# A 224-byte tile dealt first from the right end of SBUF in a hybrid SSD/pool/ConvGLU block

## Chip, cores, metric

The kernel runs on one core of a Trainium2 chip. The metric is the device time of one execution in microseconds (us), lower is better.

## The reference, cut to what matters

One decoder block on a sequence of 1024 positions of width 1024, all in float32:

```python
u = rmsnorm(h, g_norm1) * (1 + scale1) + shift1
h = h + gate1 * hybrid_mixer(u, ...)
v = rmsnorm(h, g_norm2) * (1 + scale2) + shift2
h = h + gate2 * conv_glu(v, ...)
out = rmsnorm(h, g_final)
```

`hybrid_mixer` projects u to 8224 columns, convolves and gates them, runs a chunked state-space scan beside a multi-scale pooling branch, projects each branch back to width 1024, merges the two under sigmoid gates and multiplies by `w_out`. `conv_glu` projects v to 2 x 2816 columns, convolves one half, multiplies the halves, and projects back with `w_ffn_out`.

## The kernel before, in words

**Precision.** Every large product is made of three TensorE matmuls: a float32 operand is split into a high part in float32r (ScalarE, L133, L137 or L165) and a low part, the rest (VectorE or GpSimd, L134, L138 or L166), and high x high, high x low and low x high are added in PSUM. The matmul's stationary operand is a 128x128 piece of a weight form `wf`; the moving operand is a 128x512 half of an activation tile [128, 2, 512], 2048 bytes in each partition. Products in plain float32 exist too: the sums of squares (L482, L1049), the scan's products (L740 to L832), and a few small ones.

**Stages, in order of time.** (1) norm 1 and forms of u (to about 95 us); (2) the input projection, 31 pairs of column blocks by seven Winograd-style products each (`wino_pair`, L276, matmuls in `product`, L261), with an epilogue of convolution (L562 to L575) for most of the pairs; (3) the scan in chunks of 128 positions (L710 to L832), with the pooling branch's GEMMs (L877) and the first half of the SSD output projection (L905) filled in between by a hand-written table; (4) from about 1125 us the second half of that projection (moving operand `ya`, L993), the gates, and `w_out` (moving operand `mg`, L993); (5) residual, norm 2, forms of v (L1059 to L1108); (6) the FFN input projection, 22 pairs by `wino_pair` (moving operands `x..` and `xT..`, L261); (7) the FFN output projection (moving operand `hd`, L993), and the last norm.

**Where tiles lie.** SBUF is dealt out as a stack from each end of a partition. On the left lie `const`, `wp` (weights as loaded, `wr`, their sums, and the forms `wf`), `xf` (forms of u, `xa` and `xb`; stages 1 and 2) and `xp` (`pb`, then `ya` of the first half; stage 3). On the right lie, one after the other in time, `condp`, `xpool`, `cfp` and `evp` (stages 1 and 2), `sp`, `sl`, `sl2`, `sl3` (stage 3), and from stage 4 on `hp` and `slots`, from which every `ya`, `mg`, `x..`, `xT..`, `hd`, `h`, `gt`, `o` and `fin` tile is taken:

```python
    hp = ctx.enter_context(pool("hp", side="right"))
    sq_ = ctx.enter_context(pool("slots", side="right"))
    def take(shape, dtype, name):
        n = places.pop(0)
        t = sq_.tile(shape, dtype, name=name, tag=f"q{n}")
```

The right end from which tiles are dealt is byte 229,344 of a partition, which is 895 x 256 + 224. In the program before, every right-side tile therefore begins 224 bytes past a multiple of 256 (`ev` and `edge` at 160), since all but `edge` (64 bytes) have sizes that are multiples of 256. The left-side pools `wp`, `xf` and `xp` begin on multiples of 256, and so do all their tiles. `xf` reaches from byte 77,056 to 191,744; `slots` from 77,792 to 204,768. The PSUM banks of the large products are the same six before and after stage 3.

**Order of work.** The order on every engine is the program's order, but for two weight loads in stage 3 that are given a higher priority. A tile that takes the place of another waits for that one tile's last use (`reuse_waits="tile"`).

Of the kernel before, what the change touches and what calls it, by code (L numbers as in the profile page):

```python
# [9 lines left out]
F32 = mybir.dt.float32  # L10
# [6 lines left out]
P = 128  # L17
# [68 lines left out]
def block_kernel(ctx, tc, xT, ccol_d, crow, wadn, wada, prm_d, alog, dtbias, w_in, w_dt, w_grp, w_pout, w_sout, w_out, w_fin, w_fout,  # L86
# [28 lines left out]
    mod = const.tile([P, 48], F32, name="mod")  # L115
    gs1 = const.tile([P, 8], F32, name="gs1")
    gs2 = const.tile([P, 8], F32, name="gs2")
    cond_stack = ExitStack()
    cond = cond_stack.enter_context(tc.tile_pool(name="condp", bufs=1, side="right")).tile([P, 1024], F32, name="cond")

# [1145 lines left out]
```

## Time and profile before

| | us |
|---|---|
| median of 3 runs | 2031.9 |
| lowest and highest | 2030.55, 2033.45 |
| the profiled execution's own time | 2034.22 |
| its span, first to last instruction | 2032.4 |
| PE busy in it | 1888.7 (93%) |
| VectorE, ScalarE, GpSimd busy | 1352.2, 797.1, 694.7 |

The profile is of one execution. PE is TensorE's matmul record, PEld its weight load, DVE VectorE, ACT ScalarE, POOL GpSimd, SP the engine that issues most DMAs. Matmuls are pipelined: a record lasts longer than the time until the next one begins. So a run of n matmuls back to back lasts (n - 1) intervals and one record, and the interval is best read from the starts of two runs that follow each other. L-numbers are lines of the kernel.

### The profile page before, as it was taken

To read this page: it belongs to the slowest core of one execution; us is meant where nothing else is said; L and a number is where in the kernel's file an instruction comes from. 1 tells how busy PE (TensorE), PEld (TensorE's weight loads), DVE (VectorE), ACT (ScalarE), POOL (GpSimd) and SP (SyncE) were. 2 spreads that over 40 slices of the span, in tenths; PEclk is the share of its full clock that TensorE was granted. 3 is DMA by queue.
4 is the path that set the end of the run, shared out by engine and by line. 5 is a ranking of instruction groups with operands and counts; after the bars stand their busy time and mean duration, and the time that the engine had idled before them with its cause. 6 is when DMAs were issued, how large, how long until landed. Compare 5 with 4: busy or idle time off the path is not lost.

```text
span 2032.4 us, 23730 instructions
## 1 busy us (share of the span) xinstructions
PE 1888.7 (93%) x8480; PEld 1488.4 (73%) x8480; DVE 1352.2 (67%) x1863; ACT 797.1 (39%) x1299; POOL 694.7 (34%) x499
## 2 busy tenths in 40 slices
PE   4899999999899988987789999979999999999997
PEld 1477777777788866775567787757888888888885
DVE  7899998568754578877874444688676776723324
ACT  4545444333343374435532323454333333512211
POOL 4554545454554204544654001233232322000012
PEclk8899999999999999998899999989999999999998
DMA  7133343433343577778887545412222222634212
GB/s 310 53 129 135 125 141 130 152 121 118 134 141 129 180 236 223 218 215 236 270 249 233 174 135 175 156 52 97 90 73 84 75 81 89 206 105 129 80 36 83
DMA packets 163990, 294.65 MB, mean 145 GB/s; under 512 B 13344, under 2 KB 86176, under 8 KB 163360
## 3 DMA queue, kind: packets, MB, share of 16 engines
q1 hardware_dynamic: 142368, 276.36, 41.7%
q10 hardware_dynamic: 21504, 16.78, 2.6%
q8 instruction: 66, 1.08, 0.2%
q14 instruction: 52, 0.43, 0.1%
HBM read 221.92 MB, written 71.17 MB: 144 GB/s over the span
## 4 chain that ended last, share of the span: by engine, by line
PE 65%; DVE 15%; DMA 7%; issue 5%; POOL 4%; ACT 4%; SPq 0%; ACTq 0%; DVEq 0%; POOLq 0%
PE pg L993 21%; PE bz L261 16%; PE bx L261 11%; PE bw L261 11%; DVE acc L564 4%; DMA xs<-xbc_d 2%; PE q L905 2%; DVE wf L134 1%; DVE d L731 1%; POOL sq L812 1%; POOL yv L808 1%; DMA m_d<-ht 1%; ACT acc L562 1%; POOL yv L821 1%; PE q L877 1%
## 5 line engine op out<-in xcount | busy, mean ns | idle before, releaser
L155 POOL TENSOR_TENSOR wsum<-wr 128x512 f32<-128x512 f32 x108 | 171.5, 1588 | 302.2 <-DMA wr<-in_w_fin_dram 115.7
L993 PE MATMUL pg<-hd,wf 128*128 128x512 f32 x1056 | 247.7, 397 | 0.0
L993 PEld LDWEIGHTS pg<-hd,wf 128*128 128x128 f32 x1056 | 198.7, 188 | 48.4 <-issue 1.0
L134 DVE TENSOR_TENSOR wf<-wr,wf 128x512 fp32r<-128x512 f32 x198 | 174.9, 889 | 80.5 <-ACT wf L133 80.4
L133 ACT CAST wf<-wsum 128x512 fp32r<-128x512 f32 x216 | 132.2, 618 | 194.6 <-PE bz L261 174.7
L261 PE MATMUL bz<-xT,wf 128*128 128x512 f32 x792 | 197.8, 398 | 5.6 <-ACT xT L133 5.3
L261 PE MATMUL bz<-xb,wf 128*128 128x512 f32 x744 | 184.2, 397 | 13.3 <-DVE ev L294 13.3
L133 ACT CAST wf<-wr 128x512 fp32r<-128x512 f32 x198 | 121.8, 621 | 176.6 <-PE bw L261 134.3
L261 PEld LDWEIGHTS bz<-xT,wf 128*128 128x128 f32 x792 | 149.4, 189 | 43.6 <-ACT xT L133 6.0
L261 PEld LDWEIGHTS bz<-xb,wf 128*128 128x128 f32 x744 | 140.4, 191 | 48.7 <-DVE ev L294 19.8
L1057 POOL TENSOR_TENSOR total<-total,ht 128x512 f32<-128x512 f32 x20 | 32.7, 1639 | 412.6 <-ACT ht L1056 412.1
L134 POOL TENSOR_TENSOR wf<-wsum,wf 128x512 fp32r<-128x512 f32 x62 | 90.8, 1465 | 171.3 <-ACT wf L133 171.3
L165 ACT CAST wf<-wr 128x1024 fp32r<-128x1024 f32 (+2 forms) x64 | 58.4, 914 | 224.4 <-PE pg L993 180.6
L166 DVE TENSOR_TENSOR wf<-wr,wf 128x1024 fp32r<-128x1024 f32 (+2 forms) x64 | 71.3, 1119 | 112.6 <-issue 63.7
L261 PE MATMUL bx<-x,wf 128*128 128x512 f32 x528 | 132.9, 403 | 5.4 <-ACT ht L271 5.4
L134 DVE TENSOR_TENSOR wf<-wsum,wf 128x512 fp32r<-128x512 f32 x154 | 130.1, 847 | 7.4 <-ACT wf L133 6.6
L564 DVE SCALAR_TENSOR_TENSOR acc<-cf,prm,acc 128x1023 f32<-128x1023 f32 (+2 forms) x72 | 125.2, 1756 | 6.9 <-ACT acc L562 6.9
L261 PEld LDWEIGHTS bx<-x,wf 128*128 128x128 f32 x528 | 100.8, 191 | 31.2 <-ACT ht L271 6.4
L155 POOL TENSOR_TENSOR wsum<-wr,wsum 128x512 f32<-128x512 f32 x54 | 79.8, 1478 | 104.0 <-DVE wf L134 99.7
L731 DVE TENSOR_SCALAR d<-row,dtp 128x128 f32<-128x128 f32 x256 | 88.9, 347 | 27.2 <-ACT e L703 24.5
L808 POOL TENSOR_TENSOR yv<-yv,zs 128x512 f32<-128x512 f32 x32 | 44.1, 1378 | 175.6 <-DVE yv L801 175.6
L993 PE MATMUL pg<-ya,wf 128*128 128x512 f32 x384 | 92.1, 403 | 4.2 <-ACT ya L137 4.2
(254 smaller groups left out, 3705.3 us busy)
## 6 DMA issues: line engine op xcount, KB each, us to landing
wr<-in_w_in_dram SPq DMA_DIRECT2D x64, 512.0 KB, 4.3
wr<-in_w_fin_dram SPq DMA_DIRECT2D x48, 512.0 KB, 4.1
wa<-in_wada_dram SPq DMA_DIRECT2D x32, 512.0 KB, 3.3
row<-row_d SPq DMA_DIRECT2D x32, 512.0 KB, 5.5
xbc_d<-acc SPq DMA_DIRECT2D x24, 512.0 KB, 2.6
ht<-gate_d SPq DMA_DIRECT2D x48, 256.0 KB, 4.3
hid_d<-o SPq DMA_DIRECT2D x22, 512.0 KB, 2.6
hd<-hid_d SPq DMA_DIRECT2D x44, 256.0 KB, 3.6
```

The costliest lines, as they stand in the source:

```text
L133: A.copy(dst[:, 0], src)
L134: (lo_eng or V).tensor_tensor(dst[:, 1], src, dst[:, 0].bitcast(F32), op=ALU.subtract)
L155: PL.tensor_tensor(t, a, b, op=op)
L165: A.copy(hi, r)
L166: V.tensor_tensor(lo, r, hi.bitcast(F32), op=ALU.subtract)
L261: PE.matmul(b, f[:, wi, k * P:(k + 1) * P], forms.f[x, k][:, xi], start=start and k == 0 and i == 0, stop=k == forms.n - 1 and i == 2, ski ...
L564: V.scalar_tensor_tensor(out=dst[:, k:], in0=src[:, :S - k], scalar=pcol(wname, i * taps + taps - 1 - k), in1=dst[:, k:], op0=ALU.mult, op ...
L731: V.tensor_scalar(d[:, h], q.row[:, 4 * half + h], dtp[:, 0, k:k + 1], 80.0, op0=ALU.subtract, op1=ALU.min)
L808: PL.tensor_tensor(q.yv, q.yv, q.zs, op=ALU.mult)
L905: PE.matmul(q, w[wi][:, k * P:(k + 1) * P], ys[k][:, h, xi], start=k == 0 and i == 0, stop=k == 7 and i == 2)
L993: PE.matmul(b, w[wi][:, n * P:(n + 1) * P], x[:, xi], start=first and i == 0, stop=last and i == 2)
L1057: PL.tensor_tensor(total[:, hsl(h)], total[:, hsl(h)], tmp, op=ALU.add)
```

## The change

One line is added behind the constants and ahead of the first right-side pool. It opens a pool of one buffer on the right side that stays open to the end, and allocates a tile of 56 float32 in it, 224 bytes in each partition. Nothing writes or reads this tile.

```diff
     gs2 = const.tile([P, 8], F32, name="gs2")
+
+    ctx.enter_context(tc.tile_pool(name="pad", bufs=1, side="right")).tile([P, 56], F32, name="pad")
     cond_stack = ExitStack()
     cond = cond_stack.enter_context(tc.tile_pool(name="condp", bufs=1, side="right")).tile([P, 1024], F32, name="cond")
```

## Rows read from the trace of the kernel before

**Rows 1.** The page: shares of the span in the chain that ended last
```profile
PE 65%; DVE 15%; DMA 7%; issue 5%; POOL 4%; ACT 4%; SPq 0%; ACTq 0%; DVEq 0%; POOLq 0%
PE pg L993 21%; PE bz L261 16%; PE bx L261 11%; PE bw L261 11%; DVE acc L564 4%; DMA xs<-xbc_d 2%; PE q L905 2%; DVE wf L134 1%; DVE d L731 1%; POOL sq L812 1%; POOL yv L808 1%; DMA m_d<-ht 1%; ACT acc L562 1%; POOL yv L821 1%; PE q L877 1%
```

**Rows 2.** Windows: busy us (instructions) PE, PEld, DVE, ACT, POOL; clock; DMA share, GB/s
```profile
1124.00:1309.00 185.00, 184.17 (x775) 147.14 (x776) 92.43 (x124) 63.14 (x91) 16.72 (x10) 0.99 0.48 156
1309.00:1364.00 55.00, 42.60 (x154) 30.51 (x153) 43.96 (x62) 31.95 (x55) 16.98 (x11) 0.88 0.21 67
...
1391.00:1765.00 374.00, 373.86 (x1596) 301.52 (x1597) 268.46 (x317) 148.55 (x219) 92.66 (x68) 1.00 0.27 92
1765.00:2014.00 249.00, 248.99 (x1063) 199.56 (x1062) 81.42 (x106) 55.33 (x82) 21.14 (x13) 1.00 0.31 97
```

**Rows 3.** The chain by line in the window from 1391 to 2014 us
```profile
by line: PE pg L993 39.4%; PE bz L261 26.1%; PE bw L261 17.8%; PE bx L261 16.2%; PE rr L1049 0.5%; DVE fin L1162 0.1%; DVE ht L297 0.1%; issue 0.0%
```

**Rows 4.** Timeline of PE, stage 2, left-side moving operand: start us, us, what
```profile
317.84 2.88 PE L261 MATMUL bx<-xa,wf 128*128 128x512 f32 x12
320.56 2.88 PE L261 MATMUL bz<-xa,wf 128*128 128x512 f32 x12
```

**Rows 5.** The same timeline, stage 6, right-side moving operand
```profile
1504.75 2.96 PE L261 MATMUL bw<-x,wf 128*128 128x512 f32 x12
1507.55 2.96 PE L261 MATMUL bz<-xT,wf 128*128 128x512 f32 x12
```

**Rows 6.** Timeline of PE: ya on the left (L905) and on the right (L993)
```profile
1090.44 25.87 PE L905 MATMUL q<-ya,wf 128*128 128x512 f32 x113
...
1179.69 37.26 PE L993 MATMUL pg<-ya,wf 128*128 128x512 f32 x159
```

**Rows 7.** Groups of matmuls, right-side moving operand: count | busy us, mean ns | idle before
```profile
L993 PE MATMUL pg<-hd,wf 128*128 128x512 f32 x1056 | 247.7, 397 | 0.0
L261 PE MATMUL bz<-xT,wf 128*128 128x512 f32 x792 | 197.8, 398 | 5.6 <-ACT xT L133 5.3 <-DVE xT L134 0.3
L261 PE MATMUL bx<-x,wf 128*128 128x512 f32 x528 | 132.9, 403 | 5.4 <-ACT ht L271 5.4
L993 PE MATMUL pg<-ya,wf 128*128 128x512 f32 x384 | 92.1, 403 | 4.2 <-ACT ya L137 4.2
L993 PE MATMUL pg<-mg,wf 128*128 128x512 f32 x384 | 91.4, 399 | 0.0
L261 PE MATMUL bw<-xT,wf 128*128 128x512 f32 x264 | 67.4, 400 | 1.4 <-DVE xT L134 1.4
L261 PE MATMUL bw<-x,wf 128*128 128x512 f32 x264 | 66.8, 403 | 2.1 <-DVE ht L297 2.1
```

**Rows 8.** Timeline of PE in stage 6: a run behind a wait
```profile
1326.08 12.42 PE L261 MATMUL bx<-x,wf 128*128 128x512 f32 x43 [4.70 <-ACT ht L271]
```

**Rows 9.** Groups of the other engines, left-side and right-side tiles
```profile
L133 ACT CAST wf<-wr 128x512 fp32r<-128x512 f32 x198 | 121.8, 621 | 176.6 <-PE bw L261 134.3 <-PE pg L993 15.6 <-PE bz L261 7.2
L984 ACT CAST hd<-hd 128x512 fp32r<-128x512 f32 x44 | 26.7, 620 | 23.2 <-DMA hd<-hid_d 18.1 <-PE pg L993 3.3 <-DMA wr<-in_w_fout_dram 1.2
L134 DVE TENSOR_TENSOR xa<-xtmp,xa 128x512 fp32r<-128x512 f32 x4 | 2.7, 683 | 0.0
L1103 DVE TENSOR_TENSOR h<-h,h 128x512 f32<-128x512 f32 x4 | 2.7, 682 | 0.0
L908 POOL TENSOR_TENSOR ht<-ht 128x512 f32<-128x512 f32 x16 | 20.6, 1287 | 28.4 <-DVE ht L907 12.8 <-DMA ht<-mix_d 9.0 <-issue 4.8
L808 POOL TENSOR_TENSOR yv<-yv,zs 128x512 f32<-128x512 f32 x32 | 44.1, 1378 | 175.6 <-DVE yv L801 175.6
```

**Rows 10.** Plain float32 matmuls, ns min/median/max: moving operand right (rr), left (ss)
```profile
L1049 PE MATMUL rr<-ht,ones x16: 591/593/697, 1263.6 to 2017.2; 128*128 128x512 f32 x16
L482 PE MATMUL ss<-adw,ones x12: 592/874/1222, 14.6 to 22.1; 128*128 128x512 f32 x12
```

**Rows 11.** Tile xs: its DMA's time to landing
```profile
DMA to landing us min/median/max: 2.8/4.3/9.3
```

## The prediction

> **What bounds the kernel now.** I read the chain that ended last first: 65% of the span is PE, and of its lines L993 and L261 hold 59%; VectorE has 15%, DMA 7% [rows 1]. Then I read the windows by stage. From 1124 us on PE is busy without a break, except for one stretch: 184.17 of 185 us, then 42.60 of 55 (norm 2 and the forms of v), then 373.86 of 374 (FFN input) and 248.99 of 249 (FFN output) [rows 2]. In the last two, PE lines make up over 99% of the chain [rows 3]. VectorE, the next busiest, has 268.46 of 374 us. So from 1124 to 2014 us the time is a count of matmuls times their interval, and only what changes that interval matters.
>
> The change issues nothing. It moves addresses: each right-side tile goes 224 bytes down, from 224 past a multiple of 256 onto a multiple (`ev` and `edge` from 160 past to 192 past). So the question is whether any engine's time depends on where a tile begins. The trace can answer it without the changed kernel, because left-side tiles already begin on multiples of 256: compare like instructions on the two sides.
>
> **The matmul interval.** In stage 2 the moving operand `xa` lies left. Two runs of 12 start at 317.84 and 320.56 us [rows 4]: 2.72 us for 12, or 226.7 ns each. In stage 6 it lies right, in `slots`. Two such runs start at 1504.75 and 1507.55 [rows 5]: 2.80 us, 233.3 ns each. Weights, shape, type and PSUM banks are alike; the records differ too, by the runs' 2.88 and 2.96 us.
>
> Is it the place or the stage? `ya` occurs on both sides. On the left, 113 matmuls last 25.87 us: less one record of 0.39, over 112 intervals, 227.5 ns. On the right, some 90 us later, 159 last 37.26: less 0.40, over 158, 233.3 ns [rows 6]. The ranges of bytes of `xf` and `slots` overlap almost wholly, so it is not the region either. What is left that tells the two groups apart is where in 256 bytes the 2048-byte row begins. I take 233.3 - 226.7 = 6.67 ns as the price of the unaligned start. The smaller end is 233.3 - 227.5 = 5.8 ns, from the `ya` pair; the left run it rests on ran in stage 3, beside the scan's work, so it may hold other small waits; I take the first, whose rows are undisturbed runs on both sides.
>
> **The sum.** Float32r matmuls with a right-side moving operand: 1056 + 792 + 528 + 384 + 384 + 264 + 264 = 3672 [rows 7]. All lie after 1124 us.
> - 384 + 384 (`ya`, `mg`) in the window 1124 to 1309, PE without a break: 768 x 6.67 = 5.1 us.
> - 1596 in 1391 to 1765: 10.6 us.
> - 1056 (`hd`) to 2014: 7.0 us.
> - The other 252, from 1309 to 1391, I take at nothing. There PE waits for the casts and differences of norm 2 (idle 5.3, 5.4 and 2.1 us in front of `bz`, `bx` and `bw`, [rows 7]), so a shorter matmul ends in a longer wait. If all of it counted, it would be 1.7 us more.
>
> Sum 3420 x 6.67 = 22.8 us; ends 3420 x 5.8 = 19.8 and 3672 x 6.67 = 24.5.
>
> **What hides, what is late next.** A pair in stage 6 takes 84 matmuls: 19.6 us now, 19.0 then. VectorE's work for one is 268.46 / 374 x 19.6 = 14.1 us; ScalarE and GpSimd have less. So the cover is some 5 us per pair, and PE stays the bound. All transfers together run at 92 GB/s in that stage and 97 in the next [rows 2], below the 156 of the window 1124 to 1309, in which PE didn't wait either.
>
> **All other users of right-side tiles**, at nothing: ScalarE's cast takes 621 ns on the left and 620 on the right, VectorE's difference 683 and 682 [rows 9]. GpSimd's product has 1287 ns left and 1378 right; its share of the chain is 4%, 81 us [rows 1], and 7% of that would be 5.8 us of further gain. I take zero, because GpSimd's rows hold waits for VectorE's traffic and the two stages differ in that. Plain float32 matmuls show no difference (right 591 at the least, left 592, [rows 10]), so the scan's products keep their time. In the other direction I allow 1 us for the stages before 1124, where the only event is that `ev`, also no longer at 160, is off 256 as before. No DMA is added or moved in its queue, and no wait: all right-side tiles shift together, and against left-side tiles of earlier stages none comes to lie on a tile that it did not already touch.
>
> **Forecast.** The profiled execution took 2034.22 us (span 2032.4), 2.3 above the median; 2034.22 - 22.8 = 2011.4 for a profiled one, and 2031.9 - 22.8 = 2009.1 for the median. Its own ends: 2031.9 - 24.5 = 2007.4 and 2031.9 - 19.8 = 2012.1, and 1.4 on either side for the spread of the runs before (2030.55 to 2033.45): 2006 to 2013.5.
>
> **Rivals.**
> *No change (8%).* The 6.67 ns belong to something that goes with the right side other than the start within 256 bytes, or a shift of 224 bytes is not what removes it. The changed kernel would take 2031.9 us, with 2.80 us per run of 12. The trace speaks against it by `ya` on both sides and by the overlapping byte ranges, but it holds only two values of the start, so which step matters is not shown. The Trainium skill's page "SBUF — State Buffer" (Specifications) speaks for this rival: it gives lines of 16 bytes, of which each new one costs. By that rule a row of 2048 bytes beginning 224 = 14 x 16 past a boundary crosses as many lines as an aligned one, and the change would bring nothing. The trace disagrees, by 2.80 against 2.72 us [rows 4, 5].
>
> *More than the matmuls (3%).* Transfers into and out of the right-side tiles get shorter as well. The chain holds 2% of the span in waits for `xs`, 41 us [rows 1]; if every such load landed in its least time, 2.8 us in place of the median 4.3 [rows 11], that would be 35% of it, 14 us more: 1995. Against it: the spread from 2.8 to 9.3 us is at one and the same start, so it comes from traffic. On the page "DMA: Bandwidth & Descriptors" (How a descriptor splits into AXI transactions) the Trainium skill has a descriptor that starts off a multiple of 256 bytes pay for one more transaction. No row here isolates that.
>
> *Slower (4%).* PE, quicker by 0.56 us per pair, begins to wait for VectorE's evacuations in stage 6, and its clock is cut after each wait. The price is in the trace: behind a wait of 4.70 us, 43 matmuls took 12.42 us [rows 8] where 43 intervals and a record's rest make 10.2, so 2.2 us are lost; and the stretch of such waits, 1309 to 1364, has a mean granted clock of 0.88, between full (2.4 GHz) and half (1.2), against 1.00 in 1391 to 1765 [rows 2]. Ten such cuts eat the gain of 22.8; one in each of the 22 pairs costs 48 us, net 2057. It decides from the point where VectorE's 14.1 us per pair, with waits inside, pass 19.0. Against it: the 5 us of cover.
>
> **How the numbers follow.** Forecast 85%, no change 8%, slower 4%, more 3%. The time given is the forecast's, 2009.1. The range is its own ends, with 3 us below for part of what GpSimd or DMA may add: 2003 to 2014. That holds some 80%. About 0.2%, 4 us, is what a measurement of this kernel can tell from no change. Faster by more than that: 85 + 3 = 88%; within: 8%; slower: 4%.
>
> **What would show it.** Right: runs of 12 in stage 6 start 2.72 us apart with a length of 2.88; seven matmul groups of [rows 7] sink by about 2.8% in busy time; PE busy falls by 23 to 25 us in all; everything before 1124 us keeps its times within a few us; rows of the other engines stay. The stretch from 1309 to 1391 keeps its length, with more idle PE. Wrong: an interval still at 233 ns (no change); the interval at 227 but PE idle within pairs, or a granted clock under 1.00 between 1391 and 2014 (slower, or gain lost); the gain sitting ahead of 1124 us (the cause is elsewhere).

## The result, and the profile after

The changed kernel takes 2007.53 us (median of 4 runs, 2001.23 to 2009.06), the kernel before, on the same chip, 2032.68 (4 runs). The ratio is 0.9869, 95% interval 0.9850 to 0.9888: 1.3% faster, where 2009.1 us was forecast. One run of the kernel before, beside the first four experiments, took 6487.93 us and is left out of their ratios. The profiled execution took 2009.06 us with a span of 2007.1, against 2034.22 and 2032.4 before. Lines of the changed kernel below the added one are two higher (L261 is L263, L993 is L995); each experiment's own lines shift a little in the same way.

The timeline of PE in stage 6 of the changed kernel, to be held against [rows 5] and [rows 8] (start us, length us, what):

```profile
1318.55 11.63 PE L263 MATMUL bx<-x,wf 128*128 128x512 f32 x43 [4.85 <-ACT ht L273]
...
1502.04 2.88 PE L263 MATMUL bz<-xT,wf 128*128 128x512 f32 x12
1504.76 2.88 PE L263 MATMUL bw<-xT,wf 128*128 128x512 f32 x12
```

Two runs of 12 now start 2.72 us apart and last 2.88, as on the left side before [rows 4]. Before it was 2.80 and 2.96.

Groups of matmuls of the changed kernel, those of [rows 7] (count | busy us, mean ns | idle before, released by):

```profile
L995 PE MATMUL pg<-hd,wf 128*128 128x512 f32 x1056 | 240.7, 390 | 0.0
L263 PE MATMUL bz<-xT,wf 128*128 128x512 f32 x792 | 193.3, 392 | 6.1 <-ACT xT L135 5.7 <-DVE ht L296 0.3
...
L263 PE MATMUL bx<-x,wf 128*128 128x512 f32 x528 | 129.0, 395 | 5.5 <-ACT ht L273 5.5
...
L995 PE MATMUL pg<-ya,wf 128*128 128x512 f32 x384 | 90.4, 398 | 4.2 <-ACT ya L139 4.2
L995 PE MATMUL pg<-mg,wf 128*128 128x512 f32 x384 | 89.0, 392 | 0.0
...
L263 PE MATMUL bw<-xT,wf 128*128 128x512 f32 x264 | 65.9, 395 | 1.1 <-DVE xT L136 1.1
L263 PE MATMUL bw<-x,wf 128*128 128x512 f32 x264 | 65.2, 397 | 2.1 <-DVE ht L299 2.1
```

The seven together went from 896.1 to 873.5 us, by 22.6. The waits in front of them are what they were. Where the time went by stage is read from the first start of each stage's operand, in both traces. Tile rows of the changed kernel (ns min/median/max, first start to last):

```profile
L995 PE MATMUL pg<-ya,wf x384: 387/389/793, 1121.5 to 1211.5; 128*128 128x512 f32 x192
...
L263 PE MATMUL bx<-x,wf x528: 387/389/798, 1301.9 to 1741.2; 128*128 128x512 f32 x176
...
L995 PE MATMUL pg<-hd,wf x1056: 387/389/796, 1746.8 to 1988.9; 128*128 128x512 f32 x176
```

The median record fell from 396 ns to 389 in all three. In the kernel before the same starts are 1124.8 us (`ya`), 1309.4 (`x`) and 1765.2 (`hd`), and the last `hd` starts at 2014.2. With the first `bw<-x` of the FFN input behind norm 2's waits (1391.1 before, 1383.4 after) this gives:

| stretch | before | after | difference | forecast |
|---|---|---|---|---|
| start to first `ya` | 1124.8 | 1121.5 | -3.3 | 0 |
| `ya`, gates, `mg` | 184.6 | 180.4 | -4.2 | -5.1 |
| norm 2 and forms of v | 81.7 | 81.5 | -0.2 | 0 |
| FFN input | 374.0 | 363.4 | -10.6 | -10.6 |
| FFN output | 249.0 | 242.1 | -6.9 | -7.0 |

Together -25.2 us; the spans differ by 25.3. Windows of the changed kernel over those stretches, against [rows 2] (busy us and instructions of PE, PEld, DVE, ACT, POOL; granted clock, as a share of TensorE's full clock; DMA share; GB/s):

```profile
1300.00:1355.00 55.00, 42.60 (x157) 31.66 (x156) 43.82 (x60) 31.61 (x54) 16.95 (x11) 0.91 0.21 67
1383.00:1746.80 363.80, 363.43 (x1596) 300.91 (x1597) 266.57 (x318) 148.93 (x219) 93.29 (x68) 1.00 0.27 94
1746.80:1989.00 242.20, 242.18 (x1063) 199.21 (x1062) 81.74 (x107) 55.10 (x82) 21.07 (x13) 1.00 0.31 100
```

The same 1596 matmuls take 363.43 us for 373.86, PE has no idle time to speak of, and the granted clock stays at 1.00, the full 2.4 GHz. The other engines are busy for as long as before, to within 2 us in 374.

### The profile page after: what moved, and what is told of

Read it like the earlier page. It is cut to its first block, busy times and chain, and to the rows that moved or that the text cites. A ratio compares the mean times of both kernels' runs of the same rounds, so it can differ in the third digit from the quotient of the medians.

```text
span 2007.1 us, 23730 instructions
## 1 busy us (share of the span) xinstructions
PE 1866.7 (93%) x8480; PEld 1487.6 (74%) x8480; DVE 1351.3 (67%) x1863; ACT 797.5 (40%) x1299; POOL 690.4 (34%) x499
## 4 chain that ended last, share of the span: by engine, by line
PE 63%; DVE 14%; DMA 7%; issue 6%; POOL 5%; ACT 3%; SPq 0%; ACTq 0%; DVEq 0%; POOLq 0%
PE pg L995 21%; PE bz L263 16%; PE bx L263 11%; PE bw L263 11%; DVE acc L566 4%; DMA xs<-xbc_d 1%; POOL yv L823 1%; POOL sq L814 1%; DVE d L733 1%; DVE wf L136 1%; POOL yv L810 1%; DMA m_d<-ht 1%; DMA y_d<-yv 1%; PE q L907 1%; ACT acc L564 1%
## 5 line engine op out<-in xcount | busy, mean ns | idle before, releaser
L157 POOL TENSOR_TENSOR wsum<-wr 128x512 f32<-128x512 f32 x108 | 167.8, 1554 | 291.3 <-DMA wr<-in_w_fin_dram 135.3
L995 PE MATMUL pg<-hd,wf 128*128 128x512 f32 x1056 | 240.7, 390 | 0.0
L995 PEld LDWEIGHTS pg<-hd,wf 128*128 128x128 f32 x1056 | 198.3, 188 | 41.9 <-issue 1.0
L263 PE MATMUL bz<-xT,wf 128*128 128x512 f32 x792 | 193.3, 392 | 6.1 <-ACT xT L135 5.7
L263 PE MATMUL bz<-xb,wf 128*128 128x512 f32 x744 | 184.0, 396 | 12.9 <-DVE ev L296 12.9
L263 PEld LDWEIGHTS bz<-xT,wf 128*128 128x128 f32 x792 | 149.4, 189 | 39.4 <-ACT xT L135 6.4
L263 PEld LDWEIGHTS bz<-xb,wf 128*128 128x128 f32 x744 | 140.2, 190 | 48.7 <-DVE ev L296 19.6
L167 ACT CAST wf<-wr 128x1024 fp32r<-128x1024 f32 (+2 forms) x64 | 58.4, 915 | 214.6 <-PE pg L995 184.6
L263 PE MATMUL bx<-x,wf 128*128 128x512 f32 x528 | 129.0, 395 | 5.5 <-ACT ht L273 5.5
L263 PEld LDWEIGHTS bx<-x,wf 128*128 128x128 f32 x528 | 100.0, 190 | 28.2 <-ACT ht L273 6.6
L733 DVE TENSOR_SCALAR d<-row,dtp 128x128 f32<-128x128 f32 x256 | 89.1, 348 | 25.5 <-ACT e L705 22.8
L810 POOL TENSOR_TENSOR yv<-yv,zs 128x512 f32<-128x512 f32 x32 | 42.9, 1342 | 175.2 <-DVE yv L803 175.2
L907 PE MATMUL q<-ya,wf 128*128 128x512 f32 x384 | 96.0, 404 | 0.4 <-ACT wf L167 0.4
```

The costliest lines, as they stand in the source:

```text
L157: PL.tensor_tensor(t, a, b, op=op)
L167: A.copy(hi, r)
L263: PE.matmul(b, f[:, wi, k * P:(k + 1) * P], forms.f[x, k][:, xi], start=start and k == 0 and i == 0, stop=k == forms.n - 1 and i == 2, ski ...
L733: V.tensor_scalar(d[:, h], q.row[:, 4 * half + h], dtp[:, 0, k:k + 1], 80.0, op0=ALU.subtract, op1=ALU.min)
L810: PL.tensor_tensor(q.yv, q.yv, q.zs, op=ALU.mult)
L907: PE.matmul(q, w[wi][:, k * P:(k + 1) * P], ys[k][:, h, xi], start=k == 0 and i == 0, stop=k == 7 and i == 2)
```

## The experiments

The prediction left open which property of the start counts, and whether all of the gain is the matmuls'. The expectations name the theories by letters, each with what it says. Diffs are against the changed kernel unless said otherwise. "Place" is the start of a tile's row modulo 256 bytes. In the measured lines an interval is the 95% interval of the ratio to the kernel before, run on the same chip.

### Other shifts of the right side

**e_pad32**: the right side ends up at place 192.

```diff
-    ....tile([P, 56], F32, name="pad")
+    ....tile([P, 8], F32, name="pad")
```

> The pad is 32 bytes in place of 224: right-side tiles begin 192 past a multiple of 256, that is on a multiple of 64. Theory A (the price of 6.67 ns per float32r matmul is paid when the moving row begins off a multiple of 64 bytes): intervals of 226.7 ns after 1124 us as with the pad of 224, and some 25 us faster than before, about 2007. Rival B (a multiple of 256 is needed): intervals of 233.3 ns, about 2032. Rival C (the price falls with the distance to the next multiple of 256): 64 of 256 bytes are still missing, so between 227 and 233 ns and 2010 to 2028.

Measured: 2032.26 us (10 runs) against 2035.52 of the kernel before on that chip (25 runs), ratio 0.9986, interval 0.9969 to 1.0004. Timeline of PE in its stage 6:

```profile
1514.05 2.96 PE L263 MATMUL bz<-xT,wf 128*128 128x512 f32 x12
1516.85 2.96 PE L263 MATMUL bw<-xT,wf 128*128 128x512 f32 x12
```

**e_pad128**: the same tile with `[P, 32]`; the right side at place 96.

> The pad is 128 bytes: right-side tiles begin 96 past a multiple of 256, that is 32 past a multiple of 64. Theory A: 233.3 ns and about 2032, no faster than before, though a pad of the same kind is there. Rival B: the same. Rival C: nearer to or farther from 256 than before, so another interval than 233.3. Rival D (the pad itself or the shift of the stack helps, not where the rows begin): about 2007.

Measured: 2031.09 us (10 runs), ratio 0.9980, interval 0.9963 to 0.9998. Timeline of PE in its stage 6:

```profile
1513.22 2.96 PE L263 MATMUL bx<-x,wf 128*128 128x512 f32 x12
1516.02 2.96 PE L263 MATMUL bz<-xT,wf 128*128 128x512 f32 x12
```

In both, runs of 12 start 2.80 us apart, as before the change. (The interval of e_pad128 ends just under 1, but far from 0.9869.) So neither the pad tile itself nor a shift as such brings the gain, and a multiple of 64 isn't enough.

### The left side moved off

**e_xf32**: only `xa` and `xb` move, to place 32; the right side stays at 0.

```diff
+    xf.tile([P, 8], F32, name="xpad")
```

The line stands right behind the opening of the pool `xf`.

> The pad of 224 stays, and the forms of u (left side, pool xf) are moved 32 bytes off by a tile of their own. Theory A: the 2604 matmuls of the input projection go from 226.7 to 233.3 ns, 17.4 us if all are on the path; the stage was not wholly bound by PE (575 of 595 us busy), so 11 to 17 us slower than with the pad alone, about 2018 to 2024; the stages after 1124 us keep 226.7 ns. Rival D (right-side tiles alone matter, or the side): no change against 2007.5.

Measured: 2016.73 us (4 runs), ratio 0.9904, interval 0.9871 to 0.9938. Timeline of PE in its stage 2, to be held against [rows 4]:

```profile
320.18 2.96 PE L263 MATMUL bx<-xa,wf 128*128 128x512 f32 x12
322.98 2.96 PE L263 MATMUL bz<-xa,wf 128*128 128x512 f32 x12
```

The left side now pays the 2.80, while stage 6 keeps 2.72:

```profile
1501.06 2.88 PE L263 MATMUL bx<-x,wf 128*128 128x512 f32 x12
1503.78 2.88 PE L263 MATMUL bw<-x,wf 128*128 128x512 f32 x12
```

So it is the place, not the side. The loss is smaller than the 11 to 17 us expected: 0.9904 - 0.9869, of 2032 us, is 7 us. These two intervals overlap a little, so the loss is better read in the traces. The window of stage 2 says why, first for the changed kernel, then for this one:

```profile
103.90:722.00 618.10, 599.13 (x2585) 486.21 (x2584) 453.75 (x542) 250.26 (x363) 289.70 (x184) 0.99 0.40 135
```

```profile
103.90:729.30 625.40, 611.32 (x2585) 484.15 (x2584) 448.77 (x542) 250.74 (x363) 290.78 (x184) 0.99 0.39 133
```

PE is busy 12.2 us longer, but the stage lasts 7.3 us longer: here PE has idle time (19 us in the changed kernel), and longer matmuls eat into it. Group of `bz<-xb` of this kernel, whose wait for `ev` was 12.9 us in the changed kernel:

```profile
L263 PE MATMUL bz<-xb,wf 128*128 128x512 f32 x744 | 187.2, 400 | 8.6 <-DVE ev L296 8.6
```

**e_wp32**: the weights move to place 32; `xf` and `xp` get 224 more bytes, so that they stay at 0.

```diff
+    wp.tile([P, 8], F32, name="wpad")
...
+    xf.tile([P, 56], F32, name="xpad")
...
+    xp.tile([P, 56], F32, name="ppad")
```

> The pad of 224 stays, and pool wp (weights as loaded, their sums, the weight forms, the half tiles of stage 3) is moved 32 bytes off, with xf and xp kept on multiples of 256. Theory A in its narrow form (only the moving row of a float32r matmul pays): 2007.5 within 4 us; the weight loads stay near 188 ns or go up by up to 2 ns (512 bytes are read, not 2048), hidden behind a matmul either way; the q<-wf matmuls, 96 of them with a moving row in wp, go to 233 ns, 0.6 us. Rival E (weight loads, VectorE, ScalarE, GpSimd or DMA pay for an unaligned start too): the groups of wf and wsum get longer by more than 1%, and the time is over 2012.

Measured: 2041.35 us (10 runs), ratio 1.0034, interval 1.0019 to 1.0050, slower than the kernel before. Its timeline of PE, in stages 2, 3 and 6:

```profile
319.31 2.96 PE L264 MATMUL bx<-xa,wf 128*128 128x512 f32 x12
322.11 2.96 PE L264 MATMUL bz<-xa,wf 128*128 128x512 f32 x12
...
728.65 2.89 PE L861 MATMUL q<-wf 128*128 128x512 f32 x12
...
1515.53 2.96 PE L264 MATMUL bx<-x,wf 128*128 128x512 f32 x12
1518.33 2.96 PE L264 MATMUL bz<-xT,wf 128*128 128x512 f32 x12
```

If the moving row's place alone decided, these intervals would have stayed at 2.72. Instead the matmuls with a moving row at 0 and weights at 32 pay 2.80 (the median record of their groups is 395 or 396 ns in all stages), though each of these moving rows lies on a multiple of 256. The products `q<-wf` (both operands from `wp`, both at 32) don't: (2.89 - 0.39) / 11 = 227 ns. This broke the statement on which the prediction rested and gave the next one: **what counts is whether weights and moving row have the same place**.

The weight loads keep their median of 188 ns. Rival E's sign, a time over 2012, came true, but not its cause: the groups that form `wf` take 880 and 853 ns on VectorE, for 880 and 862 in the changed kernel, and 620 and 617 on ScalarE, for 621 and 618; GpSimd's sums go both ways (1625 ns for 1554, 1508 for 1573).

### The price by itself, and other engines

**m_sweep** is a kernel of its own.

```diff
+    for name, o in MOVING:
+        burst(w0, mv[name][:, o:o + N], N, MM)
```

`MM` is 48, `w0` the weights at place 0.

> A kernel of its own that computes nothing of the reference: bursts of 48 matmuls with one weight, whose moving rows begin 0, 4, 16, 32, 48, 64, 96, 128 and 224 bytes past a multiple of 256; then float32r rows of 256 columns, plain float32, bfloat16 and weights at 0, 16 and 32; then VectorE, ScalarE and GpSimd on rows of 512 at 0, 4, 16 and 32; then transfers of 512 KB at 0, 32 and 224. Theory A (a multiple of 64): float32r bursts of 48 last the same at 0, 64 and 128, and about 0.31 us longer (47 x 6.67 ns) at 4, 16, 32, 48, 96 and 224; plain float32 the same at 0 and 32; the other engines and the transfers the same to 2%. Rival of 16-byte lines: 16, 32, 48, 96, 224 as 0, and only 4 longer. Rival of 32-byte steps: 32, 96, 224 as 0. Rival B (256): 64 and 128 longer too. For bfloat16 and 256 columns nothing is known: a row of half the bytes with the same price in lines would be 6.67 ns in 226.7 for bfloat16.

Its timeline of PE:

```profile
62.40 11.28 PE L61 MATMUL bank<-mv_at_sixteen,wt 128*128 128x512 f32 x48
73.52 11.35 PE L61 MATMUL bank<-mv_at_thirtytwo,wt 128*128 128x512 f32 x48
84.71 11.36 PE L61 MATMUL bank<-mv_at_fortyeight,wt 128*128 128x512 f32 x48
95.90 11.16 PE L61 MATMUL bank<-mv_at_sixtyfour,wt 128*128 128x512 f32 x48
...
118.11 11.36 PE L61 MATMUL bank<-mv_at_onetwentyeight,wt 128*128 128x512 f32 x48
...
172.50 20.76 PE L61 MATMUL bank<-fp_at_thirtytwo,fp_at_zero 128*128 128x512 f32 x48
193.10 10.52 PE L61 MATMUL bank<-bf_at_zero,wb 128*128 128x512 bf16 x47
203.46 10.52 PE L61 MATMUL bank<-bf_at_thirtytwo,wb 128*128 128x512 bf16 x47
```

With the weights at 0, 48 matmuls at 32, 48 or 128 last 11.35 to 11.36 us, (11.36 - 0.39) / 47 = 233.4 ns each; at 226.7 it would be 11.04. Rows at 96 and 224 last as long (11.37, 11.35), at 4 a little longer (11.52). The row at 0 has no burst of its own in this timeline, since it runs on from the warm-up; its last 51 matmuls, from 39.49 to 51.05 us, took 226.7 ns each. At 16 (231.7) and 64 (229.1) the price is in between. Theory A, with its multiple of 64, had expected 64 and 128 to be free; the rival of 16-byte lines, all but 4; rival B, with its multiple of 256, had both 64 and 128 pay. Plain float32 lasts 20.8 us at 0 and at 32, bf16 10.52 at both: at this pair of places only float32r pays, of the three types. For float32r rows of 256 columns nothing is shown: they lasted 5.91 us at 0 and 5.82 at 32, but the weight loads were busy for 11.87 of these 12 us, so a price of the matmul could hide behind them. Groups of VectorE and GpSimd in the same kernel:

```profile
L90 POOL TENSOR_TENSOR va_at_thirtytwo<-va_at_thirtytwo,vb_at_thirtytwo 128x512 f32<-128x512 f32 x8 | 10.1, 1262 | 13.2 <-ACT vb_at_thirtytwo L88 12.7
L90 POOL TENSOR_TENSOR va_at_zero<-va_at_zero,vb_at_zero 128x512 f32<-128x512 f32 x8 | 10.1, 1262 | 248.9 <-ACT vb_at_zero L88 248.3
...
L86 DVE TENSOR_TENSOR va_at_zero<-va_at_zero,vb_at_zero 128x512 f32<-128x512 f32 x8 | 5.5, 692 | 0.3
L86 DVE TENSOR_TENSOR va_at_thirtytwo<-va_at_thirtytwo,vb_at_thirtytwo 128x512 f32<-128x512 f32 x8 | 5.5, 692 | 0.3
```

GpSimd 1262 ns at both, VectorE 692, ScalarE's copy 617. Loads of 512 KB landed in a median of 4.8, 5.0 and 5.0 us at places 0, 32 and 224, stores in 4.9, 4.0 and 4.6. They ran beside each other, so a small price could hide in the traffic, but there is no order in them.

### Is part of the gain ahead of the matmuls?

**e_late** moves the pad's line to just before the pool `hp`, so that the scan's tiles stay at 224; **after_again** is the changed kernel once more, on the same chip.

```diff
-    ctx.enter_context(tc.tile_pool(name="pad", bufs=1, side="right")).tile([P, 56], F32, name="pad")
...
+    ctx.enter_context(tc.tile_pool(name="pad", bufs=1, side="right")).tile([P, 56], F32, name="pad")
     hp = ctx.enter_context(pool("hp", side="right"))
```

> The pad of 224 is opened only in front of the last two right-side pools, so that the tiles of the stages after 1124 us alone are moved and the tiles of norm 1, the input projection's epilogue and the scan begin at 224 (ev at 160) as before. Theory A: the whole gain but for what the stage of the scan showed (4.5 us between 720 and 1124 us in the one pair of traces): if that was scatter, 2007.5 within 3 us; Rival F (the scan's tiles gain by the alignment as well): 4 to 5 us slower than the change as it is, about 2012.

> The change as it is, beside the one above on the same chip: 2007 within 3 us, ratio near 0.987. The stage of the scan takes 400 to 405 us in its trace.

Measured: 2007.03 us (5 runs), ratio 0.9885, interval 0.9865 to 0.9905, and 2005.86 (5 runs), ratio 0.9872, interval 0.9847 to 0.9897. First `ya` in e_late, then in after_again (tile rows):

```profile
L995 PE MATMUL pg<-ya,wf x384: 387/389/796, 1120.9 to 1210.8; 128*128 128x512 f32 x192
```

```profile
L995 PE MATMUL pg<-ya,wf x384: 389/389/792, 1122.2 to 1211.9; 128*128 128x512 f32 x192
```

The two don't differ by more than their intervals, and the start at 1121 us comes without a shift of the scan's tiles too. From the first `q<-wf` to the first `ya` of the second half, the scan stage lasts 403.9 us before, 399.5 in the changed kernel, 403.4 in its second profile, 400.3 in e_late and 406.0 in e_pad32. So the 3.3 us ahead of 1124 are within the scatter of these traces, and the gain that the traces show lies behind it. A part of 1 or 2 us ahead of it is not excluded: the two medians differ by 1.2 us, with intervals of 4 to 5 us on either side.

### Everything at 224

**e_left224** is the kernel before with the pad on the left: weights, `xf`, `xp` and the right side all at place 224, nothing of the large products on a multiple of 256.

```diff
-    ctx.enter_context(tc.tile_pool(name="pad", bufs=1, side="right")).tile([P, 56], F32, name="pad")
...
+    ctx.enter_context(tc.tile_pool(name="pad", bufs=1)).tile([P, 56], F32, name="pad")
     wp = ...
```

> No pad on the right. Instead a tile of 224 bytes lies ahead of pool wp on the left, so that the weight forms, the forms of u and the tiles of stage 3 begin 224 past a multiple of 256, as all right-side tiles do in the kernel before; nothing of the large products lies on a multiple of 256 or of 64 any more. Theory G (a matmul runs at 226.7 ns where its weights and its moving row begin at the same place within 256 bytes, wherever that is): 226.7 ns in all stages, about 2007, as fast as the change. Theory B (both have to begin on a multiple of 256): 233.3 ns in all stages, as with the weights moved 32 bytes off, about 2041.

Measured: 2010.79 us (6 runs, 2007.98 to 2021.79), ratio 0.9915, interval 0.9892 to 0.9939. Its timeline of PE in stages 2 and 6:

```profile
317.57 2.88 PE L262 MATMUL bx<-xa,wf 128*128 128x512 f32 x12
320.29 2.88 PE L262 MATMUL bz<-xa,wf 128*128 128x512 f32 x12
...
1514.75 2.88 PE L262 MATMUL bz<-xT,wf 128*128 128x512 f32 x12
1517.47 2.88 PE L262 MATMUL bx<-x,wf 128*128 128x512 f32 x12
```

These runs start 2.72 us apart, with no row on a multiple of 256, and the median record is 390 ns in every large group of float32r matmuls. The same place is enough. Its profiled span, 2006.2 us, is as short as the changed kernel's (2007.1). Why two of its six runs took 2015.79 and 2021.79, and its ratio lies some 0.4% above the changed kernel's, its profile can't show, since it is of a run of 2008.02. That stays open.

**m_matrix** is a kernel of its own: bursts of 36 float32r matmuls over eight starts of the weights and eight of the moving row.

```diff
+    for wn, wo in AT:
+        for mn, mo in AT:
+            burst(wt[wn][:, wo // 4:wo // 4 + P], mv[mn][:, mo // 4:mo // 4 + N], MM)
```

`MM` is 36. Each start has a tile of its own, so two pairs differ in the higher bits of their addresses too.

> A kernel of its own that computes nothing of the reference: bursts of 36 float32r matmuls for each pair of a weight tile beginning 0, 16, 32, 64, 128, 224, 256 or 512 bytes past a multiple of 256 and a moving row beginning at one of the same places. Theory G: the eight pairs of equal places, and those of 0, 256 and 512 among each other, last 35 x 6.67 = 0.23 us less than the rest (8.33 against 8.56 us, from 226.7 and 233.3 ns). Theory B: only the nine pairs of 0, 256 and 512 are short. If places of 512 behave unlike 256, the period is larger than 256. Pairs with 16 may lie between (231.7 ns for the moving row and 226.7 for the weights in the sweep).

The lengths of the bursts in us, copied from its timeline (rows: start of the weights; columns: start of the moving row, bytes past a multiple of 256). 8.32 is (8.32 - 0.39) / 35 = 226.6 ns per matmul, 8.56 is 233.4:

```
weights     0    16    32    64   128   224   256   512
0        8.32  8.50  8.57  8.40  8.53  8.56  8.35  8.32
16       8.32  8.44  8.38  8.51  8.32  8.56  8.56  8.56
32       8.56  8.56  8.35  8.57  8.56  8.56  8.56  8.56
64       8.57  8.61  8.56  8.33  8.42  8.59  8.56  8.56
128      8.53  8.56  8.59  8.57  8.34  8.58  8.53  8.52
224      8.56  8.44  8.42  8.56  8.59  8.34  8.57  8.56
256      8.35  8.50  8.57  8.40  8.53  8.56  8.35  8.32
512      8.32  8.50  8.57  8.40  8.53  8.56  8.35  8.32
```

Five rows of that timeline, on and off the diagonal:

```profile
57.87 8.32 PE L44 MATMUL bank<-m_zero,w_zero 128*128 128x512 f32 x36
...
74.37 8.57 PE L44 MATMUL bank<-m_thirtytwo,w_zero 128*128 128x512 f32 x36
...
190.47 8.56 PE L44 MATMUL bank<-m_zero,w_thirtytwo 128*128 128x512 f32 x36
...
207.27 8.35 PE L44 MATMUL bank<-m_thirtytwo,w_thirtytwo 128*128 128x512 f32 x36
...
433.02 8.34 PE L44 MATMUL bank<-m_twotwentyfour,w_twotwentyfour 128*128 128x512 f32 x36
```

0, 256 and 512 behave alike, but for the row of weights at 16, and the diagonal is fast: of 14 pairs with the same place, 13 last 8.32 to 8.35. Of the 50 others 41 last 8.50 or more. The rest don't fit a plain rule: 16 with 16 lasts 8.44; weights at 16 are fast with 0 and 128 (8.32) and nearly so with 32 (8.38), but not with 256 and 512 (8.56), which are the same place as 0; 64 behind 0, 128 behind 64, and 16 and 32 behind 224 pay about a third to a half (8.40 to 8.44). In m_sweep weights at 16 with a row at 0 lasted 11.24 us, 230.9 ns, so this exception didn't repeat. So at 16 more than the two places counts; what makes the pattern isn't settled. No pair was faster than 226.6 ns.

## Why the prediction was right, and its step that was not

**The interval and the sum: right.** The price of 6.67 ns was taken from the undisturbed runs of 12, and 2.72 us stands in their place now. The stretches came out at -4.2, -10.6 and -6.9 us, for 5.1, 10.6 and 7.0. The first is short because this profile of the kernel before was 0.8 us quick there: e_pad32, e_pad128 and e_wp32, which pay in that stretch as well, all need 185.4 us for it, and 185.4 - 180.4 is 5.0. PE busy fell by 22.0 us, a little under the 23 to 25 named; the seven groups fell by 22.6, or 2.5%, for the 2.8% named. Behind 1124 us the traces thus show a gain of 21.9 us for the 22.8 forecast. That the medians differ by 25.2 is owed to what lies ahead of it, where nothing was forecast, and is scatter as far as the runs tell.

**The 252 matmuls at nothing: right.** 81.7 and 81.5 us, with the same waits in front. e_xf32 shows the same cover at work in the other direction: 12.2 us of PE time cost 7.3.

**The cover by VectorE, and the clock: right.** PE is busy for 363.43 of 363.80 us and the granted clock is 1.00. The rival with waits and clock cuts had nothing to start from: the wait at norm 2 that it was priced by stands at 4.85 us, for 4.70, and in the FFN input, where it needed new ones, PE is idle for 0.4 us in all.

**Other users at nothing: right.** The start changes neither VectorE, ScalarE nor GpSimd (m_sweep). GpSimd's busy time fell from 694.7 to 690.4 us, but e_left224, whose right side lies where it lay before, has 691.4. Its product that the prediction priced at up to 5.8 us took a mean of 1342 ns after the change for 1378, but 1342 in e_late too, where its tiles stayed at 224. The loads of `xs` landed in a median of 4.3 us before and after. One of the prediction's comparisons was weaker than it looked: in its plain float32 rows [rows 10] the weights `ones` lie at place 128, so both moving rows, at 0 and at 224, lie at another place than the weights. The pair of m_sweep, at the same and at another place, is the better ground.

**The step that failed** is this: "What is left that tells the two groups apart is where in 256 bytes the 2048-byte row begins", with its "price of the unaligned start". The 6.67 ns isn't paid for a start off a multiple of 256 but for a moving row at another place than the weights. In the trace of before the weights of all large products lay at 0, so the two statements couldn't be told apart there, and I didn't ask where the other operand lay. For this change both give the same number, which is why the time came out. That is luck: with the weights at another place than 0, the same move of the rows onto multiples of 256 would not have brought this gain, and e_wp32 is that case. The two statements part in e_wp32 (rows on multiples of 256, and slow) and e_left224 (nothing of the large products on a multiple, and fast).

**The rival of no change** had the weaker ground. By the lines of 16 bytes on the Trainium skill's page "SBUF — State Buffer" (Specifications) all shifts by 32 or 224 bytes should be alike. The trace disagrees: 2.80 us at a shift of 32, 2.72 at 224.

No version beat the changed kernel: e_left224 removes the same cost another way, and no pair of places in m_matrix took less than 226.6 ns per matmul, for the 226.7 of the changed kernel.

## What to carry to other kernels

Before moving a tile for its alignment, look up the start of both operands: for float32r matmuls of 128x512, weights and moving row at the same place modulo 256 bytes took 226.7 ns, most other pairs about 233. Here tiles were dealt from both ends of SBUF, and the right end, 224 bytes past a multiple of 256, gave every right-side tile another place than the weights, for nothing. Such a difference of 3% is invisible in busy shares, but plain in the starts of successive runs of like matmuls and in the median record (389 against 396 ns), and it was worth its full price only in the stretches where PE never waited.

## What the runs showed of the hardware

Not expected: the time of a float32r matmul of 512 columns depends on the relation of two addresses, not on one (226.6 to 227.4 ns where both lie at 0, at 32 or at 224, some 233.5 for 0 with 32); 0, 256 and 512 count as one place in seven of the eight rows of the matrix; bf16 and plain float32 show nothing of it at a start of 32 against 0; and weights at 16 bytes make exceptions in both directions (8.44 us where both lie at 16, 8.32 with rows at 0 or 128, yet 8.56 with rows at 256 or 512). The record of the weight load had a median of 187 or 188 ns for equal and unequal places alike, so the extra 6.7 ns show in the matmul's record and not in that of the load; by what mechanism, no run here shows.
